# First weight half and x tiles in another order, a longer warm-up, and a rearranged last norm in a two-layer encoder step

## The chip, the cores and the metric

The kernel runs on one core of a Trainium2 chip. The core has TensorE (PE, matrix products into PSUM), VectorE (DVE), ScalarE (ACT), GpSimd (POOL) and SyncE (SP); SP and ACT issue the DMAs, which one set of 16 DMA engines carries out. Each engine works through its own queue in order and waits on semaphores for the others. The metric is the device time of one execution in microseconds; the time shown is the median of three runs.

## The reference, cut to what matters

A two-layer encoder step on 512 new frames, 16 meta tokens and 32 frames of a running stream, 560 columns in all, with a model width of 1024 and float32 throughout. Only the first half-step block and the last norm are touched by the change:

```python
def rmsnorm(x, w):
    x32 = x.astype(jnp.float32)
    y = x32 * lax.rsqrt(jnp.mean(x32 * x32, axis=-1, keepdims=True) + RMS_EPS)
    return (y * w.astype(jnp.float32)).astype(x.dtype)

def swiglu_half(h, norm_w, w_gate, w_up, w_down):
    hn = rmsnorm(h, norm_w)
    return h + 0.5 * ((jax.nn.silu(hn @ w_gate) * (hn @ w_up)) @ w_down)
...
    for i in range(DEPTH):
        hp = swiglu_half(hp, ffn1_norm[i], ffn1_w_gate[i], ffn1_w_up[i], ffn1_w_down[i])
...
        hp = swiglu_half(hp, ffn2_norm[i], ffn2_w_gate[i], ffn2_w_up[i], ffn2_w_down[i])
...
    y_prompt = rmsnorm(hp[:, N_META:], final_norm)
    y_sample = rmsnorm(hs, final_norm)
```

Between the two half-steps of a layer stands a mixer: gated linear attention in layer 0, latent attention in layer 1.

## The kernel before, in words

**Layout.** The residual stream `h` stays in SBUF as eight tiles of 128 model rows (index m or k) by 560 columns; the last norm leaves out the meta columns and has 544. Columns are worked in two halves (hf 0 and 1), of 280 or 272. Every float32 product is made of three faster ones: each operand is split into a high part (cast on ACT, L371 for weights) and a low part (subtraction on DVE, L372), and PE makes high x high (L415), low weight x high (L416) and high weight x low (L418). A block of four row tiles by one half is therefore 12 matmuls, a down piece of eight is 24.

**The head.** The first gate/up pair (`plain_gate_up`, with `early` set) multiplies four weight quadrants, W0 to W3 in tiles `fr` (q: rows 0-511 or 512-1023 of the gate and up blocks; each is loaded as two 256 KB DMAs and split by `whole`), by four operands: `b11` (x tiles 0-3, half 0), `b21` (tiles 4-7, half 0), `b12` and `b22` (half 1). The first product is W0 x b11 into bank A, the second W1 x b21 into the same bank. `direct` makes the operands: it scales each x tile by the norm's weight on ACT (L181, high part) and makes the low part on DVE (L182). The root of the mean square is multiplied in later, so the squares (L432, L436, L437) are not in front of the products. The loads are issued in the order of the lines of `tile_stream_step`: ACT's queue has `nv` (norm weights) and the half-0 x tiles; SP's queue has W0, W1, the half-1 x tiles, W2, W3. Before all that, PE makes 11 products of a 128x128 tile of ones (L1513, two passes each), whose result is not used.

**The tail.** The last down projection works piece by piece: a piece (m, hf) is 24 matmuls into one of two buffers of PSUM bank Y, an addition into `h` on DVE (L650), and then `final(m, hf)`. The order of the pieces is (0,0) (1,0) (0,1) (1,1) (2,0) (3,0) (2,1) (3,1), then (4..7, 0), then (4..7, 1). `final` squares the piece on ACT and adds the square to `acc` on DVE; after m = 7 `net.roots` has PE sum `acc` over the partitions by three products with a column of ones (L447, two passes each) and DVE take the inverse root in eleven small steps (L482 to L490). `finish` brings the root back to all partitions by three transposes on PE (L454), and eight steps on DVE (L1544) multiply a tile by the norm's weight and the root; a store of 136 KB follows each (L1546). The eight steps of a half wait in the list `pending`; `final` of the following pieces takes three of them each. While the feed-forward block runs, `bank("s")` has no buffers of its own, and the sums and roots go to the two buffers of bank Y.

**What sets the order.** Each engine's queue is put into an order by a scheduler when the program is built, from the order of the code and what depends on what; the order of the DMAs of one engine is that of the code.

Of the kernel before, what the change touches and what calls it, by code (L numbers as in the profile page):

```python
# [18 lines left out]
P = 128  # L19
D = 1024  # L20
# [114 lines left out]
class Quads(Normed):  # L135
# [100 lines left out]
    def direct(self, op):  # L236

        m0, hf = {"b11": (0, 0), "b21": (4, 0), "b12": (0, 1), "b22": (4, 1)}[op]
        pairs = [(t[:, 0, :self.n], t[:, 1, :self.n]) for t in self.extra] if op == "b12" else self.operand(op)
        if op not in self.made:  # L240
            self.made.add(op)
            for i, (hi, lo) in enumerate(pairs):
                self.scaled_parts(hi, lo, m0 + i, hf)
        return pairs
# [84 lines left out]
class Net:  # L329
# [64 lines left out]
    def whole(self, src, pieces=1):  # L394
# [4 lines left out]
        for j in range(0, 8 * P, n):  # L399
            self.split(hf[:, j:j + n], lf[:, j:j + n], src[:, j:j + n])  # L400
        return hi, lo
# [166 lines left out]
    def plain_gate_up(self, i, l, f, xs, act, tp, between):  # L568
# [12 lines left out]
        def product(to, q, op, more=False):  # L581
            if early and not more:
                x = xs.direct(op)
            if q not in w:
                w[q] = self.whole(W.r[q], 2 if early and q == 0 else 1)
            if not early or more:
                x = xs.direct(op)
# [868 lines left out]
def tile_stream_step(ctx: ExitStack, tc: tile.TileContext, a: dict):  # L1456
# [16 lines left out]
    def x_in(k0, k1, hf):  # L1473
        c0, c1 = HALF_T[hf]
        (nc.scalar if hf == 0 else nc.sync).dma_start(net.h[:, k0:k1, c0:c1], a["xT"][:, k0:k1, c0:c1])
# [36 lines left out]
    for _ in range(11):  # L1512
# [22 lines left out]
    pending = []  # L1535

    def normed(hf, finish):
        c0, c1 = HALF_Q[hf]
        y = []

        def piece(k):
            if not y:
                y.append(finish())
            nc.vector.scalar_tensor_tensor(net.h[:, k, c0:c1], net.h[:, k, c0:c1], net.nv[:, w0 + k:w0 + k + 1],  # L1544
                                           y[0], op0=ALU.mult, op1=ALU.mult)
            (nc.sync, nc.scalar)[k % 2].dma_start(a["o_y"][:, k, c0:c1], net.h[:, k, c0:c1])  # L1546

        return [partial(piece, k) for k in range(ND)]

    def final(m, hf):  # L1550
        c0, c1 = HALF_Q[hf]
        n = c1 - c0
        net.square(net.h[:, m, c0:c1], n, hf, m == 0)
        for _ in range(min(3, len(pending))):
            pending.pop(0)()
        if m == ND - 1:
            pending.extend(normed(hf, net.roots(hf, n, D)))
# [139 lines left out]
```

## Time and profile before

| | us |
|---|---|
| median of three runs | 2053.05 (2052.42 to 2053.82) |
| the profiled execution | 2054.99 |
| its span | 2053.1 |
| PE busy, share of the span | 2006.6, 98% |
| DVE busy | 1619.7, 79% |
| ACT busy | 1009.5, 49% |
| mean granted clock of PE | 0.992 |

Read it thus: the page gives busy times by engine; the timeline gives each instruction's start, length, engine, source line, operation and operands, and in brackets how long the engine stood idle before it and what ended that; the view by windows gives the busy time of every engine in a stretch with the clock granted to PE (1.00 is full speed); the list of waits sums who waited for whom; the chain is the sequence of work that ended last. Names such as `Y<-ah,whi` read "output from inputs".

### The profile page before, as it was taken

How to read it: one execution, taken by the hardware profiler on the slowest of the kernel's cores; microseconds unless marked ns; L12 is line 12 of the kernel's file. 1: busy time of each engine (PE TensorE's matmuls, PEld its weight loads, DVE VectorE, ACT ScalarE, POOL GpSimd, SP SyncE). 2: the span in 40 equal slices, each digit the busy share in tenths (PEclk: the TensorE clock that was granted, in tenths of full speed). 3: DMA queues.
4: the chain of work that ended last, by engine and by line, in shares of the span. 5: the costliest groups of instructions: out<-in, count | busy, mean ns of one | idle time of the engine just before them, and what ended most of it. 6: DMA issues, size and time to landing. Idle time of an engine off the chain costs nothing.

```text
span 2053.1 us, 38088 instructions
## 1 busy us (share of the span) xinstructions
PE 2006.6 (98%) x15360; PEld 1975.7 (96%) x15360; DVE 1619.7 (79%) x3044; ACT 1009.5 (49%) x1811; POOL 52.6 (3%) x121
## 2 busy tenths in 40 slices
PE   9999999999998999999999999999989999999997
PEld 9999999989998999999999999999989999999997
DVE  8778788566658888788788878786798898887884
ACT  7444445365445544444455444454576565444451
POOL 0000000101110000000000000000110000000000
PEclk9999999999999999999999999999999999999998
DMA  5232322222221232323313323323111413333221
GB/s 181 74 112 83 103 93 79 70 80 70 68 85 60 96 106 78 104 88 104 103 50 100 104 93 93 99 77 97 56 56 48 129 42 106 101 93 108 85 80 56
DMA packets 91904, 180.16 MB, mean 88 GB/s; under 512 B 10240, under 2 KB 21888, under 8 KB 91728
## 3 DMA queue, kind: packets, MB, share of 16 engines
q1 hardware_dynamic: 86688, 171.91, 26.4%
q10 hardware_dynamic: 5040, 5.82, 0.9%
q8 instruction: 121, 1.98, 0.4%
q14 instruction: 55, 0.45, 0.1%
HBM read 173.69 MB, written 3.99 MB: 87 GB/s over the span
## 4 chain that ended last, share of the span: by engine, by line
PE 79%; DVE 13%; DMA 4%; ACT 2%; issue 2%; SPq 0%; POOL 0%; DVEq 0%; ACTq 0%; POOLq 0%
PE Y L418 8%; PE Y L415 8%; PE Y L416 8%; PE A L416 5%; PE A L415 5%; PE A L418 5%; DVE wlo L372 4%; PE ps L415 3%; PE B L416 3%; PE B L418 3%; PE B L415 3%; PE C L418 3%; PE C L416 3%; PE C L415 3%; PE ps L418 3%; PE ps L416 3%
## 5 line engine op out<-in xcount | busy, mean ns | idle before, releaser
L415 PE MATMUL Y<-ah,whi 128*128 128x280 f32 (+1 forms) x1408 | 374.3, 292 | 4.5 <-ACT ah L371 3.7
L416 PE MATMUL Y<-ah,wlo 128*128 128x280 f32 (+1 forms) x1408 | 373.4, 291 | 0.0
L372 DVE TENSOR_TENSOR wlo<-fr,whi 128x1024 fp32r<-128x1024 f32 (+1 forms) x303 | 365.2, 1215 | 9.6 <-ACT whi L371 9.3
L371 ACT CAST whi<-fr 128x1024 fp32r<-128x1024 f32 (+1 forms) x303 | 314.9, 1048 | 101.6 <-PE C L418 40.6
L415 PE MATMUL A<-x,whi 128*128 128x280 f32 (+1 forms) x1056 | 281.6, 292 | 3.6 <-ACT whi L371 3.3
L416 PE MATMUL A<-x,wlo 128*128 128x280 f32 (+1 forms) x1056 | 281.2, 292 | 0.3 <-DVE wlo L372 0.2
L415 PEld LDWEIGHTS Y<-ah,whi 128*128 128x128 f32 x1408 | 265.9, 189 | 5.9 <-ACT ah L371 4.7
L416 PEld LDWEIGHTS Y<-ah,wlo 128*128 128x128 f32 x1408 | 266.8, 190 | 0.0
L650 DVE SCALAR_TENSOR_TENSOR h<-Y,h 128x280 f32<-128x280 f32 (+1 forms) x320 | 141.2, 444 | 159.1 <-PE Y L418 158.4
L372 DVE TENSOR_TENSOR wlo<-raw,whi 128x512 fp32r<-128x512 f32 (+5 forms) x231 | 196.0, 850 | 75.2 <-ACT whi L371 70.5
L371 ACT CAST whi<-raw 128x512 fp32r<-128x512 f32 (+5 forms) x231 | 169.7, 736 | 166.5 <-PE ps L418 48.7
L418 PE MATMUL Y<-al,whi 128*128 128x280 f32 (+1 forms) x1408 | 233.8, 291 | 0.0
L290 DVE TENSOR_TENSOR fr<-fr 128x1024 f32<-128x1024 f32 x168 | 204.9, 1220 | 25.0 <-DMA fr<-W 22.8
L415 PEld LDWEIGHTS A<-x,whi 128*128 128x128 f32 x1056 | 199.7, 189 | 4.3 <-ACT whi L371 3.6
L416 PEld LDWEIGHTS A<-x,wlo 128*128 128x128 f32 x1056 | 199.7, 189 | 0.9 <-DVE wlo L372 0.9
L418 PEld LDWEIGHTS Y<-al,whi 128*128 128x128 f32 x1408 | 200.3, 189 | 0.0
L416 PE MATMUL B<-x,wlo 128*128 128x280 f32 (+1 forms) x704 | 186.4, 291 | 2.4 <-DVE wlo L372 2.4
L415 PE MATMUL B<-x,whi 128*128 128x280 f32 (+1 forms) x704 | 186.6, 290 | 0.0
L415 PE MATMUL C<-x,whi 128*128 128x280 f32 (+1 forms) x688 | 181.9, 290 | 0.0
L416 PE MATMUL C<-x,wlo 128*128 128x280 f32 (+1 forms) x688 | 181.8, 290 | 0.0
L418 PE MATMUL A<-x,whi 128*128 128x280 f32 (+1 forms) x1056 | 178.3, 291 | 0.0
L517 ACT COPY r<-A 128x560 f32<-128x560 f32 (+1 forms) x126 | 78.4, 623 | 165.4 <-PE A L418 163.7
(405 smaller groups left out, 4089.2 us busy)
## 6 DMA issues: line engine op xcount, KB each, us to landing
fr<-W SPq DMA_DIRECT2D x352, 256.0 KB, 3.4
raw<-W SPq DMA_DIRECT2D x80, 512.0 KB, 3.5
raw<-W SPq DMA_DIRECT2D x100, 256.0 KB, 3.0
raw<-W SPq DMA_DIRECT2D x40, 128.0 KB, 2.1
raw<-W SPq DMA_DIRECT2D x4, 384.0 KB, 3.2
h<-xT SPq DMA_DIRECT2D x2, 560.0 KB, 7.8
o_y<-h SPq DMA_DIRECT2D x8, 136.0 KB, 1.8
o_y<-h ACTq DMA_DIRECT2D x8, 136.0 KB, 1.8
```

What stands on the lines that cost most here:

```text
L290: self.net.nc.vector.tensor_tensor(r[out], r[x], r[y], op=ALU.add)
L371: self.nc.scalar.copy(hi, src)
L372: self.nc.vector.tensor_tensor(lo, src, hi.bitcast(F32), op=ALU.subtract)
L415: f(hi[:, b0 + k, :], xh[:, c], start=not more and k == 0, stop=False)
L416: f(lo[:, b0 + k, :], xh[:, c], start=False, stop=False)
L418: f(hi[:, b0 + k, :], xl[:, c], start=False, stop=k == n - 1)
L517: nc.scalar.copy(r[:, :, :n], of[:, :, :n])
L650: nc.vector.scalar_tensor_tensor(self.h[:, m, c], Y[:, :n], 0.5, self.h[:, m, c], op0=ALU.mult, op1=ALU.add)
```

## The change

At the head: W0's split no longer stands behind all four tiles of b11. `direct` gets a count and can make the first two tiles alone; `whole` can call back after each of its two halves. The x tiles 4-7 of half 0 are loaded from SP's queue instead of ACT's. The warm-up has 16 products instead of 11. In the tail: the roots of the first half are taken by the next piece's `final`; the last square (m = 7) is not added to `acc`, PE sums `acc` and that square into the same columns, which DVE has set to zero; sums and roots go to the banks A, B and C, which the down projection does not use; the norm's weight is multiplied in on ACT, tile by tile; and the multiplication by the root and the store take two tiles at a time.

```diff
-    def direct(self, op):
+    def direct(self, op, upto=4):
...
-        if op not in self.made:
-            self.made.add(op)
-            for i, (hi, lo) in enumerate(pairs):
-                self.scaled_parts(hi, lo, m0 + i, hf)
+        for i in range(upto):
+            if (op, i) not in self.made:
+                self.made.add((op, i))
+                self.scaled_parts(*pairs[i], m0 + i, hf)
         return pairs
...
-    def whole(self, src, pieces=1):
+    def whole(self, src, pieces=1, ahead=None):
...
             self.split(hf[:, j:j + n], lf[:, j:j + n], src[:, j:j + n])
+            if ahead:
+                ahead()
...
         def product(to, q, op, more=False):
-            if early and not more:
-                x = xs.direct(op)
+            if early and op == "b11" and q == 0:
+                xs.direct(op, 2)
+                w[q] = self.whole(W.r[q], 2, lambda: xs.direct(op))
+            elif early and not more:
+                xs.direct(op)
             if q not in w:
-                w[q] = self.whole(W.r[q], 2 if early and q == 0 else 1)
-            if not early or more:
-                x = xs.direct(op)
+                w[q] = self.whole(W.r[q])
+            x = xs.direct(op)
...
-        (nc.scalar if hf == 0 else nc.sync).dma_start(net.h[:, k0:k1, c0:c1], a["xT"][:, k0:k1, c0:c1])
+        (nc.scalar if k1 - k0 == 2 else nc.sync).dma_start(net.h[:, k0:k1, c0:c1], a["xT"][:, k0:k1, c0:c1])
...
-    for _ in range(11):
+    for _ in range(16):
         nc.tensor.matmul(warm[:, :P], net.ones, net.ones, start=True, stop=True)
...
-    pending = []
-
-    def normed(hf, finish):
-        c0, c1 = HALF_Q[hf]
-        y = []
+    pending, accs, tops = [], {}, {}
+    n = TQ // 2
+    first = (0, P, n - P)
+
+    def roots(hf, sq):
+
+        s = net.bank2("AB"[hf])[:, 0, :]
+        nc.vector.memset(s[:, :3], 0.0)
+        for x in (accs[hf], sq):
+            for j, c in enumerate(first):
+                nc.tensor.matmul(s[:, j:j + 1], x[:, c:c + P], net.ones[:, :1], start=False, stop=x is sq,
+                                 skip_group_check=True)
+        y, vh, t = (net.np_.tile([P, 3], F32, name=x, tag=x) for x in ("ry", "rv", "rt"))
+        net.rsqrt(y, s[:, :3], vh, t, D)
+        return y
+
+    def normed(hf, y):
+        c = slice(*HALF_Q[hf])
+        o = []
 
         def piece(k):
-            if not y:
-                y.append(finish())
-            nc.vector.scalar_tensor_tensor(net.h[:, k, c0:c1], net.h[:, k, c0:c1], net.nv[:, w0 + k:w0 + k + 1],
-                                           y[0], op0=ALU.mult, op1=ALU.mult)
-            (nc.sync, nc.scalar)[k % 2].dma_start(a["o_y"][:, k, c0:c1], net.h[:, k, c0:c1])
-
-        return [partial(piece, k) for k in range(ND)]
+            if not o:
+                if not tops:
+                    tops[0] = net.bank2("C")
+                o.append(tops[0][:, hf, :])
+                for j in (2, 0, 1):
+                    nc.tensor.transpose(o[0][:, first[j]:first[j] + P], y[:, j:j + 1].to_broadcast([P, P]), net.ident)
+            x = net.h[:, k:k + 2, c]
+            nc.vector.tensor_tensor(x, x, o[0][:, :n].unsqueeze(1).to_broadcast([P, 2, n]), op=ALU.mult)
+            (nc.sync, nc.scalar)[k // 2 % 2].dma_start(a["o_y"][:, k:k + 2, c], x)
+
+        return [partial(piece, k) for k in range(0, ND, 2)]
 
     def final(m, hf):
-        c0, c1 = HALF_Q[hf]
-        n = c1 - c0
-        net.square(net.h[:, m, c0:c1], n, hf, m == 0)
-        for _ in range(min(3, len(pending))):
+        hm = net.h[:, m, slice(*HALF_Q[hf])]
+        for _ in range(min(2, len(pending))):
             pending.pop(0)()
+        if m == 0:
+            accs[hf] = net.np_.tile([P, 280], F32, name="acc", tag="acc")[:, :n]
+            nc.scalar.activation(accs[hf], hm, AF.Square)
+        else:
+            sq = net.np_.tile([P, 280], F32, name="sq", tag="sq")[:, :n]
+            nc.scalar.activation(sq, hm, AF.Square)
+            if m < ND - 1:
+                nc.vector.tensor_tensor(accs[hf], accs[hf], sq, op=ALU.add)
+        nc.scalar.activation(hm, hm, AF.Copy, scale=net.nv[:, w0 + m:w0 + m + 1])
         if m == ND - 1:
-            pending.extend(normed(hf, net.roots(hf, n, D)))
+            if hf == 0:
+                pending.append(lambda: pending.extend(normed(0, roots(0, sq))))
+            else:
+                pending.extend(normed(1, roots(1, sq)))
```

What stands in the engines' queues, at three places. First ACT at the program's start, ahead of the second product; a row is the line, the operation, output from inputs and shape, `xN` for N in a row, and `x` and `xt` are parts of the operands. Before:

```order
L1459 DMA nv<-nv 128x67
L344 ACT_TABLE_LOAD
L344 ACTIVATE silu<-ones 128x1
L1475 DMA h<-xT 128x2x280 x2
L1475 DMA h<-xT 128x4x280
L181 ACTIVATE x<-h,nv 128x280 x4
L371 CAST whi<-fr 128x512 x2
L432 ACTIVATE acc<-h 128x280
L436 ACTIVATE sq<-h 128x280 x2
L371 CAST whi<-fr 128x1024
```

The same stretch of ACT after the change:

```order
L1463 DMA nv<-nv 128x67
L344 ACT_TABLE_LOAD
L344 ACTIVATE silu<-ones 128x1
L1479 DMA h<-xT 128x2x280 x2
L371 CAST whi<-fr 128x512 x2
L181 ACTIVATE x<-h,nv 128x280 x4
L434 ACTIVATE acc<-h 128x280
L438 ACTIVATE sq<-h 128x280 x2
L371 CAST whi<-fr 128x1024
```

Both casts of W0 (128x512 each) now stand ahead of all four casts of x, and the third load of x has left ACT's queue; on DVE the two low parts of W0 have moved ahead of the four of x in the same way. Second, SP's queue at the start, before:

```order
L392 DMA fr<-W 128x512 x4
L1475 DMA h<-xT 128x4x280 x2
L392 DMA fr<-W 128x512 x4
L1487 DMA ident<-ident 128x128
L392 DMA fr<-W 128x512 x8
```

And after, where the first x row is tiles 4-7 of half 0:

```order
L392 DMA fr<-W 128x512 x2
L1479 DMA h<-xT 128x4x280
L392 DMA fr<-W 128x512 x2
L1479 DMA h<-xT 128x4x280 x2
L392 DMA fr<-W 128x512 x4
```

That x load now stands between W0 and W1. Third, DVE at the first half's roots in the tail (L650 is the addition of a finished down piece, `rv`, `ry`, `rt` are the root's small tiles). Before:

```order
L437 TENSOR_TENSOR acc<-acc,sq 128x272
L650 SCALAR_TENSOR_TENSOR h<-Y,h 128x272
L437 TENSOR_TENSOR acc<-acc,sq 128x272
L482 TENSOR_SCALAR rv<-Y 128x3
L483 TENSOR_SCALAR ry<-rv 128x3
L488 TENSOR_TENSOR rt<-ry 128x3
```

After:

```order
L1583 TENSOR_TENSOR acc<-acc,sq 128x272
L654 SCALAR_TENSOR_TENSOR h<-Y,h 128x272 x2
L484 TENSOR_SCALAR rv<-A 128x3
L485 TENSOR_SCALAR ry<-rv 128x3
L490 TENSOR_TENSOR rt<-ry 128x3
L1583 TENSOR_TENSOR acc<-acc,sq 128x272
L491 TENSOR_TENSOR rt<-rt,rv 128x3
```

The root now follows two additions, those of (7,0) and of (4,1); no sum of the last square stands between, and the source is bank A instead of bank Y. On PE the three root products before stand behind (7,0), with four pieces to follow; the six after stand behind (4,1), with three to follow, and the transposes in both cases one piece later. At the very end PE has `L447` x3 and `L454` x3 before, and three products of `acc`, three of `sq` and three transposes after. Between the two ends the queues are the same but for line numbers.

## The prediction

> **What bounds the kernel now.** I read the page first, for the engine that carries the end:
>
> ```profile
> span 2053.1 us, 38088 instructions
> PE 2006.6 (98%) x15360; PEld 1975.7 (96%) x15360; DVE 1619.7 (79%) x3044; ACT 1009.5 (49%) x1811; POOL 52.6 (3%) x121
> PE 79%; DVE 13%; DMA 4%; ACT 2%; issue 2%; SPq 0%; POOL 0%; DVEq 0%; ACTq 0%; POOLq 0%
> ```
>
> PE is busy for 98% of the span and is 79% of the chain that ended last. The change leaves the order of all engines between the first feed-forward block's opening and the last down product as it was, so it can save only where PE stands still or runs slowly at the two ends. There the timeline comes next. At the start:
>
> ```profile
> 1.05 5.05 PE L1513 MATMUL Y<-ones 128*128 128x128 f32 x22 [1.05 <-DVE ones L343]
> 9.44 0.60 PE L415 MATMUL A<-x,whi 128*128 128x280 f32 x1 [3.34 <-ACT whi L371]
> 5.53 0.95 ACT L181 ACTIVATE x<-h,nv 128x280 fp32r<-128x280 f32 x2 [2.85 <-DMA h<-xT]
> 7.93 0.95 ACT L181 ACTIVATE x<-h,nv 128x280 fp32r<-128x280 f32 x2 [1.45 <-DMA h<-xT]
> 8.78 1.12 ACT L371 CAST whi<-fr 128x512 fp32r<-128x512 f32 x2
> ...
> 9.44:12.78 3.34, 3.22 (x12) 2.90 (x13) 3.00 (x5) 3.31 (x8) 0.00 (x0) 0.50 1.08 372
> 12.78:15.40 2.62, 2.62 (x22) 2.62 (x21) 2.62 (x7) 2.62 (x8) 0.00 (x0) 1.00 1.07 381
> ```
>
> (The last two rows are of the view by windows: stretch, length, busy time of PE, PEld, DVE, ACT and POOL, granted clock, DMA share, GB/s.) PE ends its warm-up at 6.1 and then waits 3.34 us, for ACT's cast of the weight, which stands behind four casts of x that wait for x. After that wait PE runs at a granted clock of 0.50 until 12.78.
>
> At the end I took the windows around the last norm, the list of waits, and the chain's last steps:
>
> ```profile
> 2023.80:2025.30 1.50, 0.00 (x0) 0.00 (x0) 0.88 (x2) 0.43 (x1) 0.00 (x0) 1.00 0.00 0
> 2025.30:2026.14 0.84, 0.82 (x7) 0.83 (x8) 0.00 (x0) 0.00 (x0) 0.00 (x0) 1.00 0.00 0
> 2026.14:2030.63 4.49, 4.49 (x25) 4.49 (x25) 1.78 (x11) 0.00 (x0) 0.00 (x0) 0.62 0.00 0
> 2030.63:2031.33 0.70, 0.49 (x6) 0.25 (x4) 0.50 (x2) 0.00 (x0) 0.00 (x0) 1.00 0.00 0
> 2031.33:2034.60 3.27, 3.27 (x24) 3.05 (x24) 3.15 (x8) 0.43 (x1) 0.00 (x0) 1.00 0.50 173
> 2034.60:2038.40 3.80, 3.27 (x26) 3.27 (x27) 1.29 (x3) 0.43 (x1) 0.00 (x0) 1.00 0.41 144
> 2038.40:2041.40 3.00, 3.00 (x24) 2.78 (x23) 0.88 (x2) 0.43 (x1) 0.00 (x0) 1.00 0.02 5
> ...
> PE Y L447 <- DVE acc L437: 3.1, 2, 1.5
> PE Y L415 <- DVE h L650: 0.7, 2, 0.5
> ACT sq L436 <- DVE h L650: 21.0, 6, 6.6
> ```
>
> After the last down piece of the first half, (7,0), PE stands idle for 1.50 us (for the last sum of squares), spends 0.84 us on the root products, and then needs 4.49 us for a piece that takes 3.00 us at clock 1.00. Then come the transposes and two waits for a PSUM bank, 0.7 us together.
>
> **The head.** Removed: nothing. Added: 5 warm-up products. Moved: W0's two casts go ahead of x's four on ACT, with their low parts on DVE; the 560 KB DMA of x[4:8], first half, goes from ACT's queue to SP's, ahead of W1. When the data land now, from the DMA view (issue rows, last number us to landing; first W0, then the second x tile of ACT's queue, then the second DMA of W1, issued at 2.11):
>
> ```profile
> 0.74 1.80 SPq L392 DMA_DIRECT2D fr<-W  x4
> fr<-W SPq DMA_DIRECT2D x2, 256.0 KB, 3.5
> h<-xT ACTq DMA_DIRECT2D x1, 280.0 KB, 6.2
> fr<-W SPq DMA_DIRECT2D x1, 256.0 KB, 5.6
> 4.00:8.60 4.60, 2.10 (x10) 1.82 (x9) 1.04 (x3) 1.62 (x4) 0.00 (x0) 1.00 1.05 374
> ```
>
> W0 lands before 5 us, W1 at 2.11+5.6 = 7.7, and the engines move 374 GB/s without a pause, so what goes ahead of a DMA delays it by its bytes. W1 now has 573 KB more in front: 0.573 MB at 374 GB/s is 1.5 us, so 9.2. The second x tile pair shares the engines with 1,120-byte rows of x instead of 2,048-byte rows of W; half of 374 GB/s moves its 0.287 MB in 1.5 us after the first pair's 5.4, so I put it at 6.9 instead of 7.9 (bounds 6.4, if the first pair too is through half a microsecond sooner, and 7.9, if nothing changes).
>
> Then ACT: W0 cast from about 4.2 to 5.4, x0 and x1 from 5.4 (their DMA still lands at 5.5), x2 and x3 from 6.9 to 7.8, three squares to 8.8, the cast of W1 at its landing, 9.2.
>
> ```profile
> 10.80 1.03 ACT L371 CAST whi<-fr 128x1024 fp32r<-128x1024 f32 x1
> 11.86 1.23 DVE L372 TENSOR_TENSOR wlo<-fr,whi 128x1024 fp32r<-128x1024 f32 x1 [0.24 <-ACT whi L371]
> 13.37 1.77 DVE L182 SCALAR_TENSOR_TENSOR x<-h,nv,x 128x280 fp32r<-128x280 f32 x4
> 16.08 0.29 PE L418 MATMUL A<-x,whi 128*128 128x280 f32 x1
> ```
>
> That cast was at 10.80, so ACT and, behind it, DVE are early by 1.6, the low parts of x for the second product by about 1.5: they end at 13.6 instead of 15.14. PE used the last of them at 16.08, 0.9 us after it was made, because it was behind from its slow start. Now PE begins by 7 to 8 us and is through its first 24 matmuls by 11.3 at most, before W1's low part (9.2+1.0+1.2 = 11.4); so it waits for DVE there and its lag of 0.9 falls to about 0.2. **Head: 1.5 + 0.7, 2.2 us earlier**, and from there on PE's own work sets the pace again as before. Without the slow clock PE would not have lagged: then the gain is 1.5. With W1 as late as the last x tiles it is nothing; with W1 at 8.5 it is 2.9.
>
> The warm-up has 22 passes in 5.05 us, 0.23 each. Ten more end at 8.4 at the latest, while x0 is ready at 5.9: they hold PE for up to 2.5 us, hidden behind W1, by 0.2 us in the worst phase. If W1 were there at 7.7, they would cost that wait.
>
> **The tail on PE.** The roots of the first half now come one piece later, behind (4,1), when their last square is 3 us old. The idle 1.50 goes. The sums get banks of their own, so the waits for bank Y (0.7) go. From 2023.80 to 2041.40 before spent 17.6 us. After: four pieces at 3.00 are 12.0; the root products double from 0.84 to about 1.5, since both the sum and the last square go through PE; the transposes 0.4 (0.49 to the end of the last). Together 13.9, **3.7 us less**. Of these 1.5 are the slow clock (4.49 against 3.00). What is late next is DVE's root: the eleven small steps that stand between 2043.77 and 2045.99 in the chain below, 2.2 us, and one sum of 0.4 among them, 2.6 us against the 3.0 of the piece beside it, a margin of 0.4; if that went, PE would wait for the transposes by what is over.
>
> The scaling by the norm's weight is a new ACT copy for each of 16 tiles (0.44 us like the square at 2041.97, or 0.52 like the scaled copies at 5.53), hidden by ACT's idle 21.0 us; exposed it would be 8.3.
>
> The Trainium skill ("TensorE: Matmul & The Clock Gate", section "Why this matters for your kernels") lets PE keep its full clock as long as no gap between bursts of matmuls passes some 3 us. The trace disagrees: 1.50 us of idleness and 0.84 us of one-column products were enough for the 0.62 of the next row. By that rule the 1.5 us would be no part of the gain, and the sum below 4.9.
>
> **The tail behind PE.** The last steps:
>
> ```profile
> 2041.97 0.44 ACT sq L436
> 2042.44 0.45 DVE acc L437
> 2042.93 0.84 PE Y L447 x6
> 2045.99 0.92 PE Y L454 x3
> ...
> 2046.93 3.35 DVE L1544 SCALAR_TENSOR_TENSOR h<-h,nv,Y 128x272 f32<-128x272 f32 x8 [1.00 <-PE Y L454]
> ...
> L528 DVE TENSOR_TENSOR gu<-gu,yn 128x544 f32<-128x544 f32 x44 | 31.7, 720 | 0.3
> o_y<-h SPq DMA_DIRECT2D x8, 136.0 KB, 1.8
> ```
>
> The last addition leaves the chain (2042.44 to 2042.93): 0.5 less, as PE adds the last square while the other sums are already in the bank. Eight products of 3.35 us become four on two tiles; at 720 ns with the overlap of neighbours that is 2.7, 0.65 less. But the stores are now 272 KB, four in 2.7 us, and their 1.11 MB need 3.0 us at 374 GB/s, the rate quoted above. Counted from the first product at 2046.93, before's last product ends at 2050.28 and its store lands 1.8 later, at 2052.1. Now the first product ends at 2047.65, four transfers follow one another in 3.0, and the part of the 1.8 that is no transfer, 1.4, comes behind: 2052.1 again. I take 0 for products and stores; the ends are 0.65 less, if stores go faster than that rate, and 0.4 more, if a double store lands one small transfer later. **0.5 us less.**
>
> **Sum.** 2.2 + 3.7 + 0.5 = 6.4. The profiled execution took 2054.99 (span 2053.1 and 1.9 around it), so its like after the change takes 2048.6. The median shown, 2053.05, is 1.9 lower than that execution; its two slow stretches, 0.7 at the head and 1.5 in the tail, could be the reason (the kernel between the ends has others, which the change leaves). If timed runs had neither, the change is worth 4.2 (2048.9); if all had both, 6.4 (2046.6). The gap of 1.9 speaks for few of them in the timed runs. I take a little over a third of the difference, 5.0: **2048.0 us**.
>
> **Rivals.**
> - *The timed runs never paid for the slow clock.* Both slow stretches are about as long: 3.34 us at least, and 2 x (1 - 0.62) x 4.49 = 3.41, as if the clock were set once in 3.4 us for the next 3.4. The hole of 2.34 us (1.50 and 0.84) fills such a step far enough in some executions and is cut in two in others. For it: the 1.9 between profile and median. Against: all of 2.2 us would have to be absent. Time 2048.9, half of its chance within 0.2%. Chance 0.22. The skill's same page (section "What's actually happening") has a window of 3.4 us that runs free of the kernel's start; the length agrees with the rows, and that its place changes from run to run no row here shows.
> - *All timed runs paid for both.* 2046.6. Chance 0.10.
> - *The head gives nothing:* W1, now third on SP's queue, lands with the x tiles at 11 or later, and ACT, DVE and PE stand where they stood. For it: one queue now carries nearly everything. Against: 374 GB/s do not care for the queue. 2053.05 less 2.7 on PE (2.2 and a third of 1.5) and 0.5 behind it gives 2049.9. It is also the case in which the change does not do at its first end what it says. Chance 0.14.
> - *Slower:* the 16 copies on ACT delay the casts of the last four down weights, and PE waits for them. Price 16 x 0.52 = 8.3 us, 2048.0 + 8.3 = 2056.3; it decides as soon as a cast ends after PE has finished the three pieces (9 us) between a buffer's release and its use. Against: the 21 us of ACT's idle time. Chance 0.04.
>
> **How the numbers follow.** The forecast has 0.50, with its own range 2047.0 to 2048.9. A run of this kernel is told from no change by about 0.2%, 4.1 us, so below 2048.9 is faster. Faster: nearly all of 0.50, half of 0.22, 0.10: 0.69. Slower 0.04, the rest, 0.27, the same. The range goes from both slow stretches and fast stores (2053.05 less 7.1) to no head gain and the stores' worse end (2049.9 and 0.4): 2046.0 to 2050.3.
>
> **What would show it.** In the profile after: ACT's first cast of W0 near 4.2 and of W1 near 9.2; PE's first product at 7 to 8, a wait of PE for DVE's low part of W1, the fourth low product at about 13.8 instead of 16.08; no PE wait over 0.3 us between the last nine pieces, their granted clock 1.00; twelve passes of root products; the last norm's four products in 2.7 us, and the span's end 11.2 us after the last piece, where it was 11.7 (2053.1 less 2041.4). Wrong would be: W1 landing past 10, PE waiting for the transposes, a slow clock in the tail, or the last store more than 2.6 us behind its issue.

## The result, and the profile after

| | before | after |
|---|---|---|
| median, timed side by side | 2054.62 us (20 runs, 2051.57 to 2060.21) | 2050.70 us (20 runs, 2045.74 to 2056.30) |
| ratio after / before, 95% | | 0.998 (0.9971 to 0.9988) |
| the profiled execution, its span | 2054.99, 2053.1 | 2046.69, 2044.9 |
| PE busy | 2006.6 | 2003.8 |
| mean granted clock in the profile | 0.992 | 0.995 |

The change makes the kernel 3.9 us faster between these medians (2.5 to 6.0 by the interval), 0.2%. The forecast was 2048.0, with a range of 2046.0 to 2050.3: the gain forecast, 5.0, lies inside the interval, the time does not lie in the range. The kernel before, timed 20 times, stands 1.6 us above the median of three that I had started from. The page of after has the same shape as before:

```profile
span 2044.9 us, 38114 instructions
PE 2003.8 (98%) x15382; PEld 1973.5 (97%) x15382; DVE 1617.1 (79%) x3036; ACT 1018.4 (50%) x1827; POOL 52.6 (3%) x121
PE 82%; DVE 10%; DMA 3%; ACT 2%; issue 1%; SPq 0%; POOL 0%; DVEq 0%; ACTq 0%; POOLq 0%
```

The head of after, from its timeline (start, length, engine, line, operation, tiles, count, and in brackets the idle time before and what ended it; the copy `r<-A` is the first use of the result of both first products):

```profile
1.05 5.50 PE L1517 MATMUL Y<-ones 128*128 128x128 f32 x32 [1.05 <-DVE ones L343]
...
4.12 0.62 ACT L371 CAST whi<-fr 128x512 fp32r<-128x512 f32 x1 [1.45 <-DMA fr<-W]
...
5.83 0.95 ACT L181 ACTIVATE x<-h,nv 128x280 fp32r<-128x280 f32 x2 [0.23 <-DMA h<-xT]
8.76 0.95 ACT L181 ACTIVATE x<-h,nv 128x280 fp32r<-128x280 f32 x2 [1.98 <-DMA h<-xT]
9.34 0.39 PE L417 MATMUL A<-x,whi 128*128 128x280 f32 x1 [1.98 <-ACT x L181]
10.60 1.03 ACT L371 CAST whi<-fr 128x1024 fp32r<-128x1024 f32 x1
11.66 1.23 DVE L372 TENSOR_TENSOR wlo<-fr,whi 128x1024 fp32r<-128x1024 f32 x1 [0.26 <-ACT whi L371]
...
17.00 0.63 ACT L613 COPY r<-A 128x560 f32<-128x560 f32 x1
```

W0's first cast is at 4.12, as forecast. But x2 and x3 wait for their DMA until 8.76 (forecast 6.9, at worst 7.9), and the three squares and W1's cast stand behind them on ACT: 10.60 for that cast, where 9.2 was forecast and 10.80 was before. The tail, by windows from one addition of a finished piece to the next (from (7,0) to (7,1)) and on to the last transposes; columns as before, the clock is the last but two:

```profile
2020.23:2023.23 3.00, 3.00 (x27) 3.00 (x25) 0.45 (x2) 0.95 (x2) 0.00 (x0) 1.00 0.00 0
2023.23:2027.59 4.36, 4.36 (x37) 4.36 (x37) 2.48 (x14) 0.95 (x2) 0.00 (x0) 1.00 0.00 0
2027.59:2030.95 3.36, 3.36 (x29) 3.36 (x28) 3.31 (x7) 0.96 (x2) 0.00 (x0) 1.00 0.42 142
2030.95:2033.95 3.00, 3.00 (x27) 3.00 (x25) 0.88 (x2) 0.96 (x2) 0.00 (x0) 1.00 0.62 210
2033.95:2037.90 3.95, 1.35 (x11) 1.18 (x10) 2.22 (x12) 0.95 (x2) 0.00 (x0) 1.00 0.02 6
```

PE is busy in every part of the four pieces: 3.00 + 4.36 (with the six root products) + 3.36 (with the transposes) + 3.00 are 13.72 us, where before took 17.62 (2023.82 to 2041.44). The forecast had 13.9. The chain's last steps:

```profile
2034.43 0.44 ACT sq L1581
2034.91 0.84 PE B L1549 x6
...
2037.74 0.17 DVE ry L492
2037.96 0.56 PE C L1565 x3
2038.54 0.72 DVE h L1567
```

No sum on DVE stands between the square and the products any more, and from the last addition (2033.95) to the span's end are 10.95 us against 11.65 (2041.44 to 2053.1). The two ends add up to 3.9 + 0.7 in this pair of profiles, and the head to 0.95 (`r<-A` at 17.00 against 17.95). The spans differ by 8.2: the other 2.6 come up in the middle, whose instructions are the same.

### The profile page after: what moved, and what is told of

Read it like the earlier page. It is cut to its first block, busy times and chain, and to the rows that moved or that the text cites. A ratio compares the mean times of both kernels' runs of the same rounds, so it can differ in the third digit from the quotient of the medians.

```text
span 2044.9 us, 38114 instructions
## 1 busy us (share of the span) xinstructions
PE 2003.8 (98%) x15382; PEld 1973.5 (97%) x15382; DVE 1617.1 (79%) x3036; ACT 1018.4 (50%) x1827; POOL 52.6 (3%) x121
## 4 chain that ended last, share of the span: by engine, by line
PE 82%; DVE 10%; DMA 3%; ACT 2%; issue 1%; SPq 0%; POOL 0%; DVEq 0%; ACTq 0%; POOLq 0%
PE Y L420 8%; PE Y L417 8%; PE Y L418 8%; PE A L418 6%; PE A L420 6%; PE A L417 6%; PE B L418 4%; PE B L420 4%; PE B L417 4%; PE C L420 4%; PE C L418 4%; PE C L417 4%; PE ps L417 3%; PE ps L420 3%; PE ps L418 3%; DVE wlo L372 3%
```

## The experiments

All times behind are medians; a kernel marked "once" was run a single time, with a profile. "Head" is the start of PE's 192nd product behind the warm-up (sums over the partitions and transposes are not counted), from where all kernels work alike; it comes 20.0 us after the copy `r<-A` shown above (20.3 in the two kernels that load the second x pair on SP's queue). "Tail" is the time from the addition of (7,0) to that of (7,1), "end" from there to the span's end.

| kernel | head | tail | end | time |
|---|---|---|---|---|
| before (first profile) | 37.93 | 17.62 | 11.65 | 2054.62 |
| after (first profile) | 36.98 | 13.72 | 10.95 | 2050.70 |
| head_only | 36.84 | 17.62 | 11.65 | 2056.00 (before there 2056.01) |
| tail_only | 39.61 | 13.72 | 11.30 | 2050.07 (before there 2056.01) |
| w1_before_x | 36.83 | 13.72 | 11.29 | 2055.51, once |
| second_x_sp | 35.70 | 13.72 | 11.31 | 2050.08, once |
| banks_only | 38.78 | 13.61 | 11.71 | 2052.12, once |
| late_bank_y | 36.91 | 14.17 | 11.30 | 2047.18, once |
| last_add | 37.04 | 13.02 | 11.85 | 2046.05, once |
| single_tiles | 37.18 | 13.72 | 10.97 | 2053.06, once |
| best | 35.66 | 13.02 | 10.75 | 2048.52 (before there 2055.82) |
| after_again | 36.70 | 13.72 | 11.30 | 2050.00 (before there 2055.82) |
| warm11 | 37.11 | 13.73 | 11.31 | 2045.97, once |
| before_again | 38.38 | 16.08 | 11.35 | 2052.96, once |
| before_look1 | 38.56 | 17.59 | 11.30 | 2059.61, once |
| before_look2 | 39.83 | 17.42 | 11.66 | 2057.60, once |
| before_look3 | 38.51 | 17.63 | 11.66 | 2055.62, once |
| before_look4 | 38.62 | 16.09 | 11.68 | 2056.48, once |

**The head and the tail alone.** `head_only` is the kernel before with the change's diff down to the warm-up (`direct`, `whole`, `product`, `x_in` and the 16 products); `tail_only` is the rest of that diff, from `pending` on, the last norm.

> The change's head (W0 cast first, x tiles 4-7 of half 0 on SP's queue, 16 warm-up products) on the tail of before. Theory 1 (the head is held by the second x pair, which landed at 8.74 in the profile after instead of 6.9): W1's cast again at about 10.6, the head worth 0.2 to 1.0 us, so a time 0 to 1 us under before. Theory 2 (the profile after was an unlucky head, the prediction's 2.2 holds in general): W1's cast near 9.2 and 1.5 to 2.2 us under before.

> The change's tail (roots a piece later, banks A, B, C, last square through PE, scaling by two tiles) on the head of before. Theory 1 (nearly all of the gain is in the tail): 3 to 4 us under before; from the last piece of the first half to the last of the second 13.7 us instead of 17.6, and 10.9 to the span's end instead of 11.7. Theory 2 (head and tail share it as predicted): 2.5 to 3 us under before.

The tail alone makes the kernel faster, ratio 0.9974 (0.9963 to 0.9985). That is 5.9 us between the medians (3.1 to 7.6), more than either theory had. For the head alone the ratio is 1.0 (0.999 to 1.001): an effect of 1 us and none can't be told apart by it, and one of more than 2 us is excluded for these runs. Its profile shows the head as early as in after, with W1's cast at 10.45 as in theory 1, and the tail as slow as before, clock included; `tail_only` shows the reverse. So by the profiles the two parts don't touch one another.

**Why the second x pair comes late.** Two kernels move loads of the changed one. `w1_before_x` issues W1 ahead of x 4-7 on SP's queue; `second_x_sp` takes the second pair off ACT's queue:

```diff
+    x0.first.load(1)
     x_in(4, 8, 0)
-    x0.first.load(1)
```

```diff
-        (nc.scalar if k1 - k0 == 2 else nc.sync).dma_start(net.h[:, k0:k1, c0:c1], a["xT"][:, k0:k1, c0:c1])
+        (nc.scalar if k1 == 2 else nc.sync).dma_start(net.h[:, k0:k1, c0:c1], a["xT"][:, k0:k1, c0:c1])
```

> After, with W1 loaded ahead of x tiles 4-7 on SP's queue; only SP's order changes. Theory 1 (the second x pair, alone on ACT's queue, waits while SP's 560 KB x DMA is served): it lands near 7.9 as in before, W1 near 7.7, W1's cast at 9.8 instead of 10.6 and the second product's x casts at 11.1 instead of 11.87. Theory 2 (only the bytes ahead of a DMA count, whatever its queue): the second x pair lands at 6.9 to 7.4 and W1's cast starts at 8.8 to 9.3.

> After, with the second x pair on SP's queue right behind W0 (W0, x 2-3, x 4-7, W1), ACT's queue keeping the first pair alone; the order of some later rows changes with it. Theory 1 (the pair was late because SP's large DMA was served ahead of it from the other queue): it lands at 6.4 to 6.8, x 4-7 near 8.0, W1 near 9.4, W1's cast at 9.4 to 9.5, and the low parts of the second product's x end near 13.0 instead of 14.93. Theory 2 (x of 1,120-byte rows is slow in itself): it lands past 8 again and nothing moves by more than 0.3.

With W1 first on SP's queue the pair still came to ACT at 8.61, so neither expectation of that run held; the order of these two loads on SP's queue made no difference to it. On SP's queue itself the pair is there before ACT needs it, ACT runs through all four x without a wait, and W1's cast comes 0.8 earlier than in after (9.84, where 9.4 to 9.5 was expected) although all else on that queue moved back:

```profile
6.16 1.79 ACT L181 ACTIVATE x<-h,nv 128x280 fp32r<-128x280 f32 x4
9.84 1.05 ACT L371 CAST whi<-fr 128x1024 fp32r<-128x1024 f32 x1 [0.16 <-DMA fr<-W]
```

The view of the DMA queues in the stretch in which the pair is under way, 5.70 to 8.80, says why (packets, MB and share of 16 engines; q1 is SP's queue, q10 ACT's). In after:

```profile
DMA packets 919, 1.20 MB, mean 386 GB/s; under 512 B 62, under 2 KB 664, under 8 KB 919
q1 hardware_dynamic: 659, 0.92, 80.9%
q10 hardware_dynamic: 260, 0.27, 24.4%
```

The sum is the full 386 GB/s, but ACT's queue got 0.27 of the 1.20 MB, 23% and not the half that I had counted on: 0.27 MB in 3.10 us are 87 GB/s. The kernel before showed it already: in its stretch from 4.70 to 9.00, with work on both queues, ACT's queue got 0.55 of 1.63 MB, a third:

```profile
DMA packets 1310, 1.63 MB, mean 379 GB/s; under 512 B 68, under 2 KB 1055, under 8 KB 1310
q1 hardware_dynamic: 788, 1.08, 69.2%
q10 hardware_dynamic: 522, 0.55, 36.5%
```

The Trainium skill ("DMA: Bandwidth & Descriptors", section "Queues, rings and completion order") has each DMA engine take turns between queues with work, a whole packet of several descriptors from one before the next. The rows of after show shares of 77 and 23%, so turns of equal bytes they were not; what sets the size of a turn no run here shows.

**The warm-up.** After with 11 products in place of 16:

```diff
-    for _ in range(16):
+    for _ in range(11):
```

> The changed kernel with 11 warm-up products instead of 16. Theory 1: the full clock at the head comes from the order (W0's casts first, so PE has its first products within 3 us of the warm-up's end): first product still near 6.4 to 7, no slow stretch within 20 us of the start, 192nd product at 36.8 to 37.2, nothing changed. Theory 2: the longer warm-up carries the clock over PE's wait for the second x pair: with 11 a slow stretch of 3.4 or 6.8 us stands at 7 to 10 us and the 192nd product comes at 38 to 39.6, as in the three profiles with the head of before.

Windows of that kernel from its first product to 16 us:

```profile
6.30:9.30 3.00, 0.95 (x4) 0.59 (x4) 1.04 (x3) 0.83 (x3) 0.00 (x0) 0.99 1.07 388
9.30:12.64 3.34, 3.20 (x13) 3.20 (x14) 2.71 (x5) 3.34 (x9) 0.00 (x0) 0.50 1.09 369
12.64:16.00 3.36, 3.36 (x27) 3.36 (x27) 3.36 (x9) 3.36 (x10) 0.00 (x0) 1.00 1.06 382
```

The slow clock is back, as theory 2 had it, and yet the head is at 37.11, within the spread of the kernels with 16 products (36.70 to 37.18), as theory 1 had it. The longer warm-up does keep the clock up, and in this one execution that is worth 0.2 us (37.11 less 36.94, the mean of six profiles with the whole new head): in after PE waits twice for 0.3 us for W1's operands, and in `warm11` the slow clock takes up that slack. What moves the head is the rest of the change there. PE's first product comes at 6.3 to 7.2 with the new order of the casts and at 9.4 to 9.9 with the old one; what the new queue of x tiles 4-7 adds to it was not run apart.

**Which part closes the hole in the tail.** `banks_only` is the kernel before with sums in the banks A and B and transposes in C, nothing else. `late_bank_y` is after with both back in bank Y.

```diff
...
-        s = self.bank("s")
+        s = self.bank2("AB"[half])[:, 0, :] if ffn else self.bank("s")
...
-            out = self.bank("s")
+            out = self.tops[0][:, half, :] if ffn else self.bank("s")
```

```diff
-        s = net.bank2("AB"[hf])[:, 0, :]
+        s = net.bank("s")
...
-                o.append(tops[0][:, hf, :])
+                o.append(net.bank("s"))
```

> The kernel before, with one part of the tail's change alone: the sums of squares go to banks A and B and the transposed roots to bank C, instead of to bank Y; when they are taken, and what sums the last square, stays as in the kernel before (the scheduler then puts the three root products 12 matmuls into the next piece, since nothing but the last sum of squares orders them). Measured from the addition of piece (7,0) to that of (7,1), which was 17.6 us before and 13.7 after the change. Theory 1: the hole came from the shared bank, whose next piece could not go past the roots; with banks of their own PE fills the wait with the next piece's products, so 12.0 + 0.84 + 0.5, 13.4 to 13.9 us, and no slow clock there. Theory 2: the roots must also be taken a piece later, or DVE's chain (last sum, 11 small steps, 2.6 us) is late for the transposes and PE waits: 14.5 us or more, with a wait of PE for DVE of 1 us or more. The head is that of before, so the time is 2.5 to 5 under the kernel before by theory 1 and 0 to 2 by theory 2.

> The changed kernel with its sums and roots back in bank Y, so of the tail's parts only the delay by a piece, the sum of the last square on PE and the scaling remain. From the addition of (7,0) to that of (7,1): theory 1 (delay is enough to close the hole of 1.5, and the banks are worth the 0.7 us of waits for bank Y only) 13.7 + 0.7, 14.2 to 14.8 us and no slow clock; theory 2 (each piece after a root stands behind the root's reading of bank Y by DVE, 2.2 us of small steps, so the holes only move): 15.5 to 18 us, PE waiting over 1 us for DVE at one place, and a slow stretch there in some executions.

The four windows from (7,0) to (7,1) in `banks_only`:

```profile
2024.75:2028.84 4.09, 3.96 (x33) 3.78 (x32) 2.27 (x11) 0.43 (x1) 0.00 (x0) 1.00 0.00 0
2028.84:2032.36 3.52, 3.46 (x29) 3.28 (x28) 3.19 (x11) 0.43 (x1) 0.00 (x0) 1.00 0.20 69
2032.36:2035.36 3.00, 3.00 (x26) 3.00 (x25) 2.02 (x7) 0.43 (x1) 0.00 (x0) 1.00 0.73 255
2035.36:2038.36 3.00, 2.96 (x24) 2.74 (x22) 0.89 (x3) 0.43 (x1) 0.00 (x0) 1.00 0.10 36
```

The sum is 13.61, as short as with the whole change (theory 1), though with three root products where the whole change has six; with three of them and the roots a piece later (`last_add`, below) it is 13.02. With a bank of its own for the sums, the scheduler puts the root products twelve matmuls into the next piece, and the hole is gone though nothing is taken a piece later. The delay alone closes it as well: `late_bank_y` takes 14.17, a little under the 14.2 to 14.8 of theory 1, 0.45 more than after. Either takes most of the hole away by itself, and the other is worth another half microsecond; the change has both. Neither kernel has a slow stretch there in its one execution.

**The end.** `last_add` lets DVE add the last square again, so that PE has three root products; `single_tiles` goes back to products and stores of one tile.

```diff
...
-            if m < ND - 1:
-                nc.vector.tensor_tensor(accs[hf], accs[hf], sq, op=ALU.add)
+            nc.vector.tensor_tensor(accs[hf], accs[hf], sq, op=ALU.add)
```

```diff
-            x = net.h[:, k:k + 2, c]
-            nc.vector.tensor_tensor(x, x, o[0][:, :n].unsqueeze(1).to_broadcast([P, 2, n]), op=ALU.mult)
-            (nc.sync, nc.scalar)[k // 2 % 2].dma_start(a["o_y"][:, k:k + 2, c], x)
+            x = net.h[:, k, c]
+            nc.vector.tensor_tensor(x, x, o[0][:, :n], op=ALU.mult)
+            (nc.sync, nc.scalar)[k % 2].dma_start(a["o_y"][:, k, c], x)
...
```

> The changed kernel, but DVE adds the last square again and PE makes three root products instead of six in each half. Theory 1 (the sum of the prediction): the end behind the last addition is 0.4 to 0.6 us longer than the 10.95 us of the changed kernel, 11.35 to 11.55, and PE's root products of the first half fall from 1.5 to 0.75, so (7,0) to (7,1) is 13.0 instead of 13.7; the two cancel to 0.2 us. Theory 2: the six products are not faster than the sum, since half of them wait for the last square anyway: the end is 10.9 to 11.1 and the whole 0.7 faster.

> The changed kernel, with the last norm's product and its store by one tile again (eight of 136 KB in place of four of 272 KB in each half). The prediction put this part at 0, since the larger store lands later by what the larger product saves. Theory 1 (that balance): from the last addition to the span's end 10.8 to 11.2 us (10.95 after). Theory 2 (the store is what counts): the last store lands 1.8 instead of 2.7 us behind its issue, and the end comes at 10.3 to 10.6. Theory 3 (DVE and the issues count): eight products need 3.35 instead of 2.6 us, the last store still takes 2.2 or more, 11.3 to 11.8. DVE has twice the instructions in the last pieces; if that delays the additions, (7,0) to (7,1) is longer than 13.9.

These ends can't be read against the 10.95 of after's first profile, and that is a trap of the expectations. The three last transposes, in the timeline of after and then of `last_add`:

```profile
2037.96 0.54 PE L1565 MATMUL C<-ident,ry 128*128 128x128 f32 x3 [2.22 <-DVE ry L492]
```

```profile
2036.96 0.90 PE L1564 MATMUL C<-ident,ry 128*128 128x128 f32 x3 [2.22 <-DVE ry L492]
```

PE is idle at the end, its clock drops there in every profile, and in after's first profile it dropped just behind the transposes instead of ahead of them: 0.36 us. Five other profiles with the same end have 11.29 to 11.31. Against 11.30, `last_add` is 0.55 longer at the end and 0.70 shorter in the tail (theory 1), and `single_tiles` is 0.33 shorter, so the larger tiles do not break even, they cost 0.33. The stores of one tile on ACT's queue are under way 2.0 us at the end, where the large ones of after take 2.5; DVE needs 2.87 for eight products against 2.61 for four (timeline of `single_tiles`, then its DMA view and that of after, both from the last addition on):

```profile
2045.01 2.87 DVE L1567 TENSOR_TENSOR h<-h,C 128x272 f32<-128x272 f32 x8 [0.99 <-PE C L1565]
```

```profile
o_y<-h ACTq DMA_DIRECT2D x4, 136.0 KB, 2.0
```

```profile
o_y<-h ACTq DMA_DIRECT2D x2, 272.0 KB, 2.5
```

**The parts put together.** `best` is after with the second x pair on SP's queue, one tile per product and store, and, in the first half alone, the last square added on DVE. To the two diffs that it takes over comes

```diff
-        for x in (accs[hf], sq):
+        xs_ = (accs[hf], sq)[:1 + hf]
+        for x in xs_:
...
-            if m < ND - 1:
+            if m < ND - 1 or hf == 0:
                 nc.vector.tensor_tensor(accs[hf], accs[hf], sq, op=ALU.add)
```

It was timed beside after itself, whose second timing is `after_again`.

> Three findings put together on top of the changed kernel: the second x pair of the first half on SP's queue (so that one queue carries it, x 4-7 and the weights), the last norm's product and store by one tile again, and in the first half alone DVE adds the last square (three root products there; in the second half PE sums it, six). Worked out from the runs before: 1.3 us less at the head (192nd product at 35.7 instead of 37.0), 0.7 less between the additions of (7,0) and (7,1) (13.0 instead of 13.7), 0.3 less behind the last addition (10.6 to 11.0, as the clock of the last transposes falls). Theory 1: the parts add up, 2.3 us under the changed kernel timed in the same call (its times scatter by 2.4 us, so 0.5 to 4 under it). Theory 2: they do not, because the eight small products on DVE or the fuller queue give one of them back: the head then stands at 37 or (7,0) to (7,1) at 13.7, and the time within 0.8 us of the changed kernel.

> The changed kernel itself once more, beside the kernel before on another chip's call. Theory 1: what the timed runs gain is the sum of the pieces that the profiles show, with the slow clock of both ends in nearly all runs of the kernel before: head 1.8 (mean of three profiles with the head of before, 38.8 us at the 192nd product, against 37.0), tail 3.9, behind it 0.4, 6.1 us, ratio 0.997. Theory 2: part of it is given back in the middle, as the first 20 runs say: 3.9 us, ratio 0.998 or above. Theory 1 also has no slow stretch within 20 us of the start and none between the additions of (7,0) and (7,1), and 13.7 us between those.

All three parts are in the profile of `best`: head 35.66, tail 13.02, end 10.75, which are 1.0 + 0.7 + 0.55 less than in `after_again`, 2.3 as expected. That sum is partly luck: the head gave 1.0 where 1.3 was expected, and of the 0.55 at the end 0.2 is the clock, which fell in the middle of the last transposes (0.70 us for them, against 0.91 in `after_again` and `single_tiles`). Its median is 1.5 below that of `after_again`, its ratio to before is 0.9968 (0.9957 to 0.998) against 0.9975 (0.9963 to 0.9987). It is ahead of both kernels by its medians, but the intervals of the two overlap: the times can't tell 2.3 us from less. `after_again` gained 5.8 us between medians, near the 6.1 of theory 1, but its interval (2.7 to 7.6) holds theory 2's 3.9 too.

**How often before pays for the slow clock.** Five more profiles of the kernel before, unchanged.

> The kernel before, one more profile of it. Theory 1 (its two holes at the ends always bring the slow clock): a slow stretch within 20 us of the start, and one between the additions of (7,0) and (7,1), which then are 17.0 to 18.2 us apart. Theory 2 (the clock's step cuts the holes in two in a fair part of the executions): one of the two stretches is missing, and the additions are 15.9 to 16.4 us apart if it is the one in the tail.

> The kernel before, the first of four more profiles of it. Theory 1 (the forecast's: few executions pay for the slow clock at both ends): in at least two of the four the 192nd product comes before 37.6 us (the clock full from 6 on) and the additions of (7,0) and (7,1) stand 15.9 to 16.4 us apart. Theory 2 (nearly all executions pay): the 192nd product comes at 37.9 to 39.7 in all four, and the additions stand 17.0 to 18.2 us apart in at least three.

> As for the first of the four looks: theory 1 has the 192nd product before 37.6 us and 15.9 to 16.4 us between the additions of (7,0) and (7,1) in at least two of the four; theory 2 has 37.9 to 39.7 in all and 17.0 to 18.2 us in at least three.

> As for the first of the four looks: theory 1 has the 192nd product before 37.6 us and 15.9 to 16.4 us between the additions of (7,0) and (7,1) in at least two of the four; theory 2 has 37.9 to 39.7 in all and 17.0 to 18.2 us in at least three.

> As for the first of the four looks: theory 1 has the 192nd product before 37.6 us and 15.9 to 16.4 us between the additions of (7,0) and (7,1) in at least two of the four; theory 2 has 37.9 to 39.7 in all and 17.0 to 18.2 us in at least three.

The window from the addition of (7,0) to the next, in `before_look3` and in `before_look4`:

```profile
2024.46:2031.47 7.01, 5.51 (x32) 5.52 (x33) 2.66 (x13) 0.43 (x1) 0.00 (x0) 0.76 0.00 0
```

```profile
2026.81:2032.28 5.47, 3.97 (x32) 3.98 (x33) 2.68 (x13) 0.43 (x1) 0.00 (x0) 1.00 0.00 0
```

Both have the hole of 1.5; only the first has the slow clock behind it, 1.54 us. With `head_only`, whose tail is that of before, five of seven profiles have it (mean of the seven tails: 17.15). At the head all eight profiles with the old order (`tail_only` and `banks_only` have it too) run their first products slowly, and the first profile, at 37.93, is the earliest of the eight: they go up to 39.83, 38.78 in the mean. The profiles `before_look1` to `before_look4` thus give theory 2, heads late in all (39.83 a little past its 39.7) and the tail slow in three of four; `before_again` is one of the two without it in the tail, as its own theory 2 had it.

## Why the prediction missed, point by point

**The step that failed is the base.** It reads: "The median shown, 2053.05, is 1.9 lower than that execution; its two slow stretches, 0.7 at the head and 1.5 in the tail, could be the reason". They are not. All eight profiles of the old head and five of seven of the old tail have those stretches, so the timed runs paid for most of it. The 1.9 was scatter: over the timings beside after and `after_again` (20 and 23 runs) before has a median of 2055.26 and a standard deviation of 2.6, and a median of three such runs is easily 2 us off. A base of 2055.26 with the forecast gain of 5.0 is 2050.3, against 2050.68 for the 31 runs of after. Of the 2.7 us between 2048.0 and the first 2050.70, the base makes 1.6 and the gain of that pair, 3.9 instead of 5.0, the other 1.1. The range had no room for this, since both of its ends were counted from the same 2053.05. The rival "the timed runs never paid" fell with the base: its gain of 4.2 is inside what the times allow (below), and its picture of the hole cut in two holds (see "The clock"), but that happens in two of seven profiles of the tail and not in all. "All paid for both" comes closest to what the profiles show, though its gain of 6.4 is just above what the times allow and its time stands on the same low base.

The scatter has a source in the records. Here are the mean granted clocks of `before_again` and of `before_look1`:

```profile
core 0: 2051.1 us, clock 0.994
```

```profile
core 0: 2057.7 us, clock 0.991
```

The records of the second show eight slow steps of 3.4 us between the two ends, those of the first five, and one more in the tail; the two kernels are the same. In the tail one such step costs 1.5 us (17.6 against 16.08 between the additions), so four make about 6 of the 6.6 us by which the spans differ. One such step in the middle of `before_look1`:

```profile
747.70:751.10 3.40, 3.40 (x17) 3.40 (x17) 3.01 (x6) 0.44 (x1) 0.00 (x0) 0.51 0.53 154
```

Over all eighteen profiles the stretch between head and tail, whose work is the same in all, lasts 1982.0 to 1991.9 us and holds four to nine slow steps; a straight line through them has 1.5 us for each step and leaves a scatter of 1.2. The timed runs agree: the longer ones have the lower mean clock (correlation -0.83 in the first 20 runs of after, -0.80 in the 23 of before). After's two profiles have four and five of these steps between the ends, before's first profile five. One step, 1.5 us, is thus the larger part of the 2.6 by which the first pair differs in its middle; the rest stays open, and so does what brings these steps.

**The gain was about right.** Worked out by the profiles' means: head 38.78 to 36.94 (six profiles with the whole new head), 1.8; tail 17.15 to 13.72, 3.4; end 11.56 (seven) to 11.24 (six), 0.3: 5.6. Timed, with both timings put together, the means differ by 5.1, give or take 1.2 (from standard deviations of 2.7 and 2.6 over 31 and 43 runs). The forecast took 5.0. How it divides the times do not confirm: `head_only` gained nothing between its medians, and the 1.8 of the profiles is close to the most that its interval allows.

**Head, 2.2 forecast, 1.8 measured, from other terms than given.** Of the 1.5 for earlier data 0.2 came in the first pair (W1's cast at 10.60 instead of 10.80) and 0.45 in the mean (11.01 in the eight profiles, 10.56 in the six). The step "half of 374 GB/s moves its 0.287 MB in 1.5 us" was wrong: ACT's queue got under a quarter, and the trace of before had shown a third. W1 itself landed at 9.4, near the 9.2 forecast, but its cast stood behind the squares of the late pair. And the lag of PE behind its data, which I had at 0.7 from the first profile, is what is left, about 1.4 in the mean, since that profile is the best of eight heads. Two errors cancelled, which is luck.

**Tail, 3.7 forecast, 3.9 in the first pair, 3.4 in the mean.** Right in each term: 12.0 for four pieces, 1.4 for the root products, 0.4 for the transposes, no wait for a bank, clock 1.00 in all ten profiles that take the roots a piece later. The margin of 0.4 for DVE's root held: the transposes wait for nothing. The slow clock's 1.5 belongs in the sum in five executions of seven.

**End, 0.5 forecast, 0.3 in the mean,** and the 0.7 of the first pair was half luck with the clock (above). The sum of the last square is worth 0.55 (`last_add`), as forecast. Products and stores, put at 0, cost 0.2: the transposes' start to the span's end is 7.10 us before and 7.30 in `tail_only`, both with 0.9 us for the transposes. That is inside the bounds given, 0.65 less to 0.4 more. The last store landed 2.7 after its issue, just past the 2.6 that I had named as a sign of it.

**The copies on ACT** cost nothing: ACT's busy time in each of the four pieces is 0.95 of 3.00 us or more, and the rival that had them delay the weights is out. **"The head gives nothing"** is out too: W1 did not wait for the last x tiles, though its cast was nearly as late as if it had.

**The clock.** What the prediction could only guess, a clock set once in 3.4 us, the records settle. In each of the eighteen profiles all changes of the granted clock, from the first to the one at the very end, stand whole multiples of 3.413 us apart, to within 0.004 us over some 597 steps. Where the first of them stands behind the program's start differs between executions (3.9 to 14.0 us). In the old tail PE makes no full product for 2.22 us, from the end of piece (7,0) to the first product of the next piece; how much of that falls into one step of this grid decides:

| profile of the old tail | PE without a full product | most of it in one step | slow step behind it |
|---|---|---|---|
| before | 2023.79 to 2026.01 | 2.22 | yes, from 2026.64 |
| head_only | 2025.97 to 2028.20 | 2.22 | yes, from 2028.91 |
| before_look1 | 2028.82 to 2031.04 | 2.22 | yes, from 2031.16 |
| before_look3 | 2024.42 to 2026.65 | 2.21 | yes, from 2027.85 |
| before_look2 | 2026.63 to 2028.85 | 1.93 | yes, from 2030.33 |
| before_again | 2023.62 to 2025.85 | 1.68 | no |
| before_look4 | 2026.77 to 2029.00 | 1.22 | no |

The border lies between 1.7 and 1.9 us of the 3.41; if the grid may fall anywhere, that makes half to two thirds of the executions slow there, an estimate from these figures. The rule from the Trainium skill ("TensorE: Matmul & The Clock Gate", section "Why this matters for your kernels") about gaps of some 3 us, weighed in the prediction, doesn't hold here, since 2.2 us were enough in five of seven. The window of 3.4 us of the same page of the Trainium skill (section "What's actually happening"), which runs free of the kernel's start, agrees with the grid and its changing place.

## What to carry to other kernels

Take the base from as many runs as the forecast's precision needs, and before explaining a gap between a profile and a median, ask whether the runs scatter by as much. A load that must be early belongs on the queue that gets the bandwidth, not on the one that is empty, and the trace of the kernel at hand shows which that is. A short hole on the engine that bounds the kernel can cost more than its length: here 2.2 us brought another 1.5 of slower clock in five executions of seven. A bank of its own for a small side result let the scheduler close it.

## What the runs showed of the hardware

The records show a granted clock of 1.00 until the first change is recorded, and that isn't always so. In `before_again`, `before_look1` and `before_look3` no slow step is recorded at the head, yet the products stand 0.23 us apart up to 13.7 to 13.9 and 0.13 just behind (timeline of `before_again`):

```profile
13.42 0.43 PE L415 MATMUL A<-x,whi 128*128 128x280 f32 x1
13.65 0.33 PE L416 MATMUL A<-x,wlo 128*128 128x280 f32 x1
13.82 0.29 PE L415 MATMUL A<-x,whi 128*128 128x280 f32 x1
13.95 0.29 PE L416 MATMUL A<-x,wlo 128*128 128x280 f32 x1
```

So PE ran at half its pace from the start, and the first change recorded is the one to the full clock. In after, too, the 32 passes of the warm-up began 0.23 apart and went on at half of that from 4.6; when that happens differs between executions (4.1 to 6.4 in the profiles with 16 products). Two queues with work didn't share the DMA engines evenly: 77 and 23% in after, 66 and 34% in before. And a large store that takes 2.5 us at the very end takes longer while the last pieces run: over both halves of after the medians are 3.5 and 3.7 (DMA view of the whole kernel), which costs nothing, as nobody waits for them:

```profile
o_y<-h SPq DMA_DIRECT2D x4, 272.0 KB, 3.5
o_y<-h ACTq DMA_DIRECT2D x4, 272.0 KB, 3.7
```
